# Three output tiles by token halves before the second norm, low parts of its odd tiles on GpSimd, final results written in place

## The chip, the core and the metric

The kernel runs on one core of a Trainium2 chip. The engines are named as in the profile: PE (TensorE, matrix products; PEld is its weight load), DVE (VectorE), ACT (ScalarE), POOL (GpSimd) and SP (SyncE, which issues the DMAs). The metric is the device time of one execution in microseconds (us). Three runs of the kernel before took 1318.2, 1317.3 and 1318.23 us: median 1318.2.

## The reference, cut to what matters

One layer over 512 latent tokens of width 1024 and 256 context tokens: a modulated RMSNorm, two parallel token mixers (a bidirectional state-space scan and windowed attention), a gated merge, then a second modulated RMSNorm and a gated feed-forward with a convolution over tokens, and a final RMSNorm. The change touches the last third:

```python
out_lat = (g_ssd * (y_ssd @ w_o_ssd) + g_att * (y_att @ w_o_att)) @ w_out
x = x + gt1 * out_lat                                   # out stage
h = modulate(x, norm2_g, sh2, sc2)                      # second norm: rmsnorm * (1 + scale) + shift
u = dwconv_centred(h @ w_up, conv_w, conv_b)            # up stage, 2 * 2816 columns
a, b = u[..., :2816], u[..., 2816:]
x = x + gt2 * ((silu(a) * b) @ w_down)                  # down stage
return rmsnorm(x, final_g)                              # final norm
```

An RMSNorm divides each token by the root of the mean square over its 1024 features, so nothing of it can be finished before the last feature of that token is there.

## The kernel before, in words

Activations lie transposed in SBUF: features on the 128 partitions (8 tiles of 128 for width 1024, 22 for 2816), the 512 tokens along the free axis. `HALF` cuts the tokens into two halves of 256.

**Split products.** Each fp32 product is made of three matmuls of rounded parts, high and low: wh·xh, wh·xl, wl·xh (`gemm`, L187, L188, L190, 512 columns each; `half_gemm`, L1073 to L1075, the same for a token half of 256 columns). A weight piece of 512 KB comes by a DMA that SP issues (L140, tile `wraw`, three buffers), ACT rounds it to `whi` (L144) and DVE subtracts for `wlo` (L145), two buffers each. `run` walks a program of steps and loads the pieces one ahead of the step that uses them. `ELSEWHERE` names pieces whose two parts go to a tile of their own; before, that is the out piece 7, in the memory of the dead tile `yh0`.

**Order.** A scheduler orders each engine's instructions; each engine runs its queue in order and waits on semaphores. Where `manual_schedule` stands for PE (`out_last`, `up_step` with t == 0, `down_last`), PE's order is the program's own. Temporaries come from rings of 512-column buffers: `ta` 3, `tb` 2, `tc` 2, `te` 2 (L111). PSUM has three banks `acc` for products and five banks `mis`.

**RMSNorm.** Squares of the tiles are summed on ACT and DVE (`add_square`, or `half_squares` on L1087 for one token half), over partitions by one-column matmuls (`rms_sums`, L229). `rms_root` adds the epsilon (DVE, L237) and takes the power -1/2 (POOL, L238); `rms_spread` copies each token's factor to all partitions by two PE transposes of 128 columns (L244) into a `mis` bank.

**Out stage.** `out_step` makes out tile o for all 512 tokens: x row load into `te` (L1104), product, DVE adds the residual (L1110), square added to `q2`. The steps 0 to 5 are woven with the last six modulation steps. `vectors` follows (small columns, matmuls L464). `out_last` makes tiles 6 and 7 in token halves, in the order o6 and o7 of half 0, o6 and o7 of half 1, with the residual on L1135; the `q2` sums of a half stand behind its o6. The root of half 0 stands behind the k step 5 (counted from 0) of o6 in half 1, the spread of half 0 behind the k step 1 of o7 in half 1.

**Second norm and up step 0.** `norm2_k(k, u)` normalizes tile k of half u: DVE writes xr = x · a · factor into a `tb` buffer (L1145, reads the spread bank in PSUM), ACT writes the high part of xr + shift (L1146), DVE writes the low part (L1147). Up step 0 works tile by tile (`product`, L1185): in half 0 both weight pieces of the step for each k, with the root of half 1 behind k = 3 and its spread behind k = 5; in half 1 first all eight k of the first piece, then all eight of the second. From step 1 on the up steps are plain `gemm`s.

**The end.** `down_last` makes the last down tile in token halves. `finish(u)` scales all eight tiles of half u by the spread factor (DVE, L1244, from PSUM; in half 1 the tiles 5 and 6 on POOL, L1242, from an SBUF copy of the factor that ACT makes on L1236) into `ta` buffers, and SP sends them in five pieces, (0,1), (2,3), (4), (5,6), (7), from L1248. For half 0 that starts beside the last products; for half 1 it is the end of the kernel. L1261 is the last residual.

Of the kernel before, what the change touches and what calls it, by code (L numbers as in the profile page):

```python
# [18 lines left out]
P = 128  # L19
# [20 lines left out]
def raw(ap):  # L40
    return ap.bitcast(F32)
# [3 lines left out]
def tile_hybrid_layer(  # L45
# [67 lines left out]
    def tmp(tag):  # L113
        return tpool.tile([P, 512], F32, tag=tag, name=tag, bufs=TMP[tag])
# [980 lines left out]
    def last_piece():  # L1095
        t = cp.tile([P, 2, 1024], F32R, tag="yh0", name="wlast")
        return t[:, 0, :], t[:, 1, :]

    ELSEWHERE["out", 7] = last_piece

    def out_step(o):
        def fn(w):
# [9 lines left out]

        return [("out", o)], fn

    def out_last(w6, w7):
        xt = [tmp("te") for _ in range(2)]
        for i in range(2):
            nc.sync.dma_start(xt[i], xT[3, :, i * L : (i + 1) * L])
        pf = F["pf"] = misb()
        F["r2"] = []  # L1120

        def root():
            F["rs2"] = half_root(pf, F["sq2"], 0)

        def spread():
            F["r2"].append(rms_spread(F["rs2"], 2))

        with tc.manual_schedule(engines={mybir.EngineType.PE}):
            for u, z in enumerate(HALF):
                for i, w in enumerate((w6, w7)):  # L1130
                    ps = accb()
                    half_gemm(ps, mh, ml, z, w, 8, 0, 8, {} if u == 0 else {1: spread} if i else {5: root})
                    if i == 0:
                        half_sums(pf, q2, u)
                    V.scalar_tensor_tensor(  # L1135
                        x1[1][:, 2 + i, z], ps[:, :HL], g1h[:, 6 + i : 7 + i], xt[i][:, z], ALU.mult, ALU.add
                    )
                F["sq2"] = half_squares([x1[1][:, 2 + i, z] for i in range(2)])

    h2h, h2l = mh, ml  # L1140
# [1 line left out]
    def norm2_k(k, u):  # L1142
        a, s, z = a2[:, k : k + 1], mod2[:, 8 + k : 9 + k], HALF[u]
        xr = tmp("tb")[:, :HL]
        V.scalar_tensor_tensor(xr, x1[k // 4][:, k % 4, z], a, F["r2"][u][:, :HL], ALU.mult, ALU.mult)  # L1145
        S.activation(h2h[:, k, z], xr, AF.Identity, bias=s)  # L1146
        V.scalar_tensor_tensor(h2l[:, k, z], xr, s, raw(h2h[:, k, z]), ALU.add, ALU.subtract)  # L1147

    def close_c1():
        c1pool.close()  # L1150
# [25 lines left out]
    def up_step(t):  # L1176
        def fn(wa, wb):
            pa, pb = accb(), accb()
            if t == 0:

                with tc.manual_schedule(engines={mybir.EngineType.PE}):
                    def product(ps, w, k, u):
                        c, z, st, en = slice(k * P, (k + 1) * P), HALF[u], u == 0 and k == 0, k == KT - 1
                        for v, y in ((0, h2h), (0, h2l), (1, h2h)):
                            T.matmul(  # L1185
                                ps[:, z], w[v][:, c], y[:, k, z],
                                start=st and v == 0 and y is h2h, stop=en and v == 1, skip_group_check=True,
                            )
# [36 lines left out]
    def down_last(*w):  # L1225

        pf = misb()
        for u in range(2):
            half_sums(pf, q3, u)
        scaled, r = {}, {}  # L1230

        def finish(u, r3):
            z = HALF[u]
            if u:
                r3s = tmp("tc")[:, :HL]
                S.copy(r3s, r3[:, :HL])  # L1236

            for cs in ((0, 1), (2, 3), (4,), (5, 6), (7,)):
                t = tmp("ta").rearrange("p (a b) -> p a b", a=2)
                for v, c in enumerate(cs):  # L1240
                    if u and c in scaled:
                        G.tensor_tensor(t[:, v, :], scaled[c], r3s, ALU.mult)  # L1242
                    else:
                        V.scalar_tensor_tensor(  # L1244
                            t[:, v, :], x1[c // 4][:, c % 4, z], col(V_FG, c), r3[:, :HL], ALU.mult, ALU.mult
                        )
                n = len(cs)
                nc.sync.dma_start(out[cs[0] * P : (cs[0] + n) * P, z].rearrange("(a p) t -> p a t", a=n), t[:, :n, :])  # L1248
                if cs[0] == 2:
                    yield  # L1250

        def root():
            r["s"] = half_root(pf, r["sq"], 0)

        def spread():
            r["f"] = finish(0, rms_spread(r["s"], 2))
            next(r["f"])

        def add(u):
            xo = x1[1][:, 3, HALF[u]]  # L1260
            V.scalar_tensor_tensor(xo, ps[u][:, :HL], mod2[:, 31:32], xo, ALU.mult, ALU.add)  # L1261
            r["sq"] = half_squares([xo])

        for i, c in enumerate((5, 6)):
            scaled[c] = tmp("te")[:, :HL]
            S.activation(scaled[c], x1[1][:, c % 4, HALF[1]], AF.Copy, scale=col(V_FG, c))
        ps = [accb(), accb()]
        with tc.manual_schedule(engines={mybir.EngineType.PE}):
# [7 lines left out]
            for _ in finish(1, rms_spread(r["s"], 2)):  # L1276
                pass

    run(
# [92 lines left out]
```

## Time and profile before

| what | value |
|---|---|
| median of three runs | 1318.2 us (1317.3 to 1318.23) |
| the profiled execution's own time | 1317.22 us |
| its span, first to last instruction | 1315.4 us |
| mean granted clock of PE | 0.985 |
| DMA moved | 168.65 MB |
| out tile 5, start of its product | 910.51 us |
| `out_last`, first product | 916.76 us |
| up step 0, first product | 930.34 us |
| up step 1, first product | 949.69 us |
| last residual of half 1 (L1261) | 1303.07 us |

Times within the profile count from the span's start. The busy shares are averages over stages with different limits. A line of a timeline has the start, the duration, the engine, the line of the kernel, the operation, what it writes and reads, its shape, and in brackets the engine's idle time before it and what ended that; "x2" joins two that follow each other. A row of waits has the waiting engine, tile and line, what it waited for, the total in us, how often, and the longest.

### The profile page before, as it was taken

To read this page: it belongs to the slowest core of one execution; us is meant where nothing else is said; L and a number is where in the kernel's file an instruction comes from. 1 tells how busy PE (TensorE), PEld (TensorE's weight loads), DVE (VectorE), ACT (ScalarE), POOL (GpSimd) and SP (SyncE) were. 2 spreads that over 40 slices of the span, in tenths; PEclk is the share of its full clock that TensorE was granted. 3 is DMA by queue.
4 is the path that set the end of the run, shared out by engine and by line. 5 is a ranking of instruction groups with operands and counts; after the bars stand their busy time and mean duration, and the time that the engine had idled before them with its cause. 6 is when DMAs were issued, how large, how long until landed. Compare 5 with 4: busy or idle time off the path is not lost.

```text
span 1315.4 us, 17187 instructions
## 1 busy us (share of the span) xinstructions
PE 1270.1 (97%) x6434; PEld 1028.7 (78%) x6434; DVE 912.7 (69%) x1457; ACT 640.5 (49%) x1182; POOL 133.3 (10%) x104
## 2 busy tenths in 40 slices
PE   4989999999999999999999999999999999999996
PEld 2777777787778878778787787888888888888886
DVE  4578887888666588888888756776677767773333
ACT  4376666666535456475574654223444444442221
POOL 0000000000000024333443430000000000000000
PEclk8998999999999999999999999999999999999998
DMA  7612222211236235444455658767133433333331
GB/s 287 234 33 80 73 80 65 79 67 57 88 112 186 95 93 135 158 112 129 145 123 190 168 166 280 248 204 249 41 116 115 131 104 114 117 110 93 99 89 65
DMA packets 86931, 168.65 MB, mean 128 GB/s; under 512 B 6784, under 2 KB 42112, under 8 KB 86848
## 3 DMA queue, kind: packets, MB, share of 16 engines
q1 hardware_dynamic: 86848, 167.56, 40.9%
q8 instruction: 50, 0.82, 0.3%
q14 instruction: 33, 0.27, 0.1%
HBM read 150.62 MB, written 16.91 MB: 127 GB/s over the span
## 4 chain that ended last, share of the span: by engine, by line
PE 87%; DVE 6%; ACT 3%; issue 1%; DMA 1%; SPq 0%; POOL 0%; DVEq 0%; ACTq 0%; POOLq 0%
PE acc L187 21%; PE acc L188 21%; PE acc L190 21%; PE score L560 2%; PE pt L584 2%; PE mis L924 2%; PE mis L931 2%; PE mis L837 2%; PE po L589 2%; DVE wlo L145 1%; PE po L590 1%; PE mis L855 1%; ACT ta L485 1%; PE mis L765 1%; PE acc L332 1%
## 5 line engine op out<-in xcount | busy, mean ns | idle before, releaser
L145 DVE TENSOR_TENSOR wlo<-wraw,whi 128x1024 fp32r<-128x1024 f32 (+1 forms) x163 | 206.1, 1265 | 133.7 <-ACT whi L144 131.5
L144 ACT CAST whi<-wraw 128x1024 fp32r<-128x1024 f32 (+1 forms) x163 | 168.9, 1037 | 230.5 <-PE acc L188 199.2
L187 PE MATMUL acc<-hlh,whi 128*128 128x512 f32 (+1 forms) x512 | 212.0, 414 | 0.4 <-ACT whi L144 0.4
L190 PE MATMUL acc<-hlh,wlo 128*128 128x512 f32 (+1 forms) x512 | 203.3, 397 | 2.2 <-DVE wlo L145 2.2
L188 PE MATMUL acc<-hll,whi 128*128 128x512 f32 (+1 forms) x512 | 203.5, 398 | 0.0
L187 PE MATMUL acc<-mh,whi 128*128 128x512 f32 x384 | 149.6, 390 | 0.0
L190 PE MATMUL acc<-mh,wlo 128*128 128x512 f32 x384 | 149.4, 389 | 0.0
L188 PE MATMUL acc<-ml,whi 128*128 128x512 f32 x384 | 149.4, 389 | 0.0
L187 PEld LDWEIGHTS acc<-hlh,whi 128*128 128x128 f32 (+1 forms) x512 | 96.7, 189 | 22.1 <-issue 4.1
L190 PEld LDWEIGHTS acc<-hlh,wlo 128*128 128x128 f32 (+1 forms) x512 | 96.3, 188 | 22.1 <-DVE wlo L145 2.9
L188 PEld LDWEIGHTS acc<-hll,whi 128*128 128x128 f32 (+1 forms) x512 | 96.7, 189 | 20.4 <-issue 4.1
L190 PEld LDWEIGHTS acc<-mh,wlo 128*128 128x128 f32 x384 | 72.1, 188 | 15.1
L187 PEld LDWEIGHTS acc<-mh,whi 128*128 128x128 f32 x384 | 72.1, 188 | 15.0
L188 PEld LDWEIGHTS acc<-ml,whi 128*128 128x128 f32 x384 | 72.1, 188 | 14.7
L839 POOL TENSOR_TENSOR st<-st,eT 128x512 f32<-128x512 f32 x24 | 32.8, 1368 | 458.0 <-ACT st L857 444.6
L737 ACT ACTIVATE ta<-acc,half 128x512 f32<-128x512 f32 (+1 forms) x66 | 46.6, 706 | 41.0 <-PE acc L190 41.0
L567 DVE CUSTOM_DVE_ANT_0 p<-score,winm,nsink 128x512 f32<-128x512 f32 (+1 forms) x64 | 52.0, 813 | 18.8 <-PE score L560 17.3
L571 ACT ACTIVATE p<-p,mneg 128x512 f32<-128x512 f32 (+1 forms) x64 | 49.9, 779 | 31.2 <-DVE mneg L567 31.0
L238 POOL TENSOR_TENSOR rs<-ms,phalf 128x2 f32<-128x2 f32 (+1 forms) x7 | 5.5, 790 | 541.0 <-DVE ms L237 541.0
L187 PE MATMUL acc<-fh,whi 128*128 128x512 f32 x154 | 60.0, 390 | 0.0
L190 PE MATMUL acc<-fh,wlo 128*128 128x512 f32 x154 | 59.9, 389 | 0.0
L188 PE MATMUL acc<-fl,whi 128*128 128x512 f32 x154 | 59.9, 389 | 0.0
(309 smaller groups left out, 2766.1 us busy)
## 6 DMA issues: line engine op xcount, KB each, us to landing
wraw<-wup SPq DMA_DIRECT2D x44, 512.0 KB, 3.5
fb<-cs_d SPq DMA_DIRECT2D x32, 512.0 KB, 6.7
wraw<-wm SPq DMA_DIRECT2D x32, 512.0 KB, 3.7
wraw<-wx SPq DMA_DIRECT2D x24, 512.0 KB, 3.6
wm<-wm SPq DMA_DIRECT2D x16, 512.0 KB, 5.5
wraw<-wz SPq DMA_DIRECT2D x16, 512.0 KB, 3.5
wraw<-wg SPq DMA_DIRECT2D x16, 512.0 KB, 3.6
wraw<-wos SPq DMA_DIRECT2D x16, 512.0 KB, 4.7
```

The lines of the kernel that those rows point to most:

```text
L144: S.copy(hi[:, :n], r[:, :n])
L145: V.tensor_tensor(lo[:, :n], r[:, :n], raw(hi[:, :n]), ALU.subtract)
L187: T.matmul(ps, wh, xh[:, k0 + k, :], start=a, stop=False)
L188: T.matmul(ps, wh, xl[:, k0 + k, :], start=False, stop=False)
L190: T.matmul(ps, wl, xh[:, k0 + k, :], start=False, stop=b)
L560: T.matmul(ps[:, o : o + w], Q[h][:, b * P : (b + 1) * P], k[:, j, z[0] * P : z[0] * P + w], start=v == 0 and o % 512 in (0, P), stop=v == ...
L567: V.tensor_tensor_reduce(p[:, :n], ps[:, o0 : o0 + n], m, op0=ALU.add, op1=ALU.min, scale=1.0, scalar=nsink[:, h : h + 1], accum_out=mn,)
L571: S.activation(p[:, :n], p[:, :n], AF.Exp, bias=mn, scale=-1.0, accum_out=den[:, i : i + 1])
L584: T.transpose(pt[:, i * P : (i + 1) * P], pts[i][:, c * P : (c + 1) * P], ident)
L589: T.matmul(po, vst[:, t, j, :], pth, start=c == 0, stop=False)
L737: S.activation(o[:, :n], ps[:, :n], AF.Identity, scale=hcol(base_w, stride + i), bias=hcol(base_b, i))
L839: G.tensor_tensor(h8(n), h8(s), bc64(eT[:, z0 : z0 + 8, c]), ALU.mult)
```

## The change

1. **Out stage.** Out tile 5 leaves the woven steps and joins `out_last`, which now makes o5, o6, o7 of half 0, then o5, o6, o7 of half 1. The three weight pieces lie in tiles of their own (`yh0` to `yh2`). The three x rows are loaded into `ld` buffers. The square of o5 is added to `q2` half by half; the `q2` sums of a half stand behind k = 2 of its o7. The root of half 0 stands behind k = 5 of o5 in half 1, its spread behind k = 4 of o6 in half 1.
2. **Second norm.** For odd k the low part is made by POOL: ACT writes xr + shift a second time, unrounded, into a `ta` buffer (L1159 after), and POOL subtracts the high part (L1160 after). Even k stay on DVE. In up step 0 the order of the three matmuls becomes wh·xh, wl·xh, wh·xl, so the low part is used last.
3. **The end.** The final results are written in place over `x1`, no longer into `ta` buffers, and sent from there. For half 1 the factor is spread twice, into two banks: one for DVE, one for ACT's copy.

On the engines' queues the scheduler follows with: the three out weights one behind the other on SP's queue, the weight splits of o5, o6, o7 and of up step 0 ahead of the first xr, and in half 1 of the norm two xr followed by one low part on DVE.

```diff
-    ELSEWHERE["out", 7] = last_piece
+    for o in (5, 6, 7):
+        ELSEWHERE["out", o] = piece_in("yh%d" % (o - 5))
...
-    def out_last(w6, w7):
-        xt = [tmp("te") for _ in range(2)]
-        for i in range(2):
-            nc.sync.dma_start(xt[i], xT[3, :, i * L : (i + 1) * L])
+    def out_last(*w):
+        xt = [cp.tile([P, L], F32, tag="ld", name="ld", bufs=3) for _ in range(3)]
+        for i, o in enumerate((5, 6, 7)):
+            nc.sync.dma_start(xt[i], xT[o // 2, :, (o % 2) * L : (o % 2 + 1) * L])
...
-                for i, w in enumerate((w6, w7)):
+                for i in range(3):
+                    after = {}
+                    if u == 1:
+                        after = {0: {5: root}, 1: {4: spread}}.get(i, {})
+                    if i == 2:
+                        after[2] = lambda u=u: half_sums(pf, q2, u)
                     ps = accb()
-                    half_gemm(ps, mh, ml, z, w, 8, 0, 8, {} if u == 0 else {1: spread} if i else {5: root})
+                    half_gemm(ps, mh, ml, z, w[i], 8, 0, 8, after)
+                    x = x1[1][:, 1 + i, z]
+                    V.scalar_tensor_tensor(x, ps[:, :HL], g1h[:, 5 + i : 6 + i], xt[i][:, z], ALU.mult, ALU.add)
                     if i == 0:
-                        half_sums(pf, q2, u)
-                    V.scalar_tensor_tensor(
-                        x1[1][:, 2 + i, z], ps[:, :HL], g1h[:, 6 + i : 7 + i], xt[i][:, z], ALU.mult, ALU.add
-                    )
+                        sq = half_squares([x])[0]
+                        V.tensor_tensor(q2[:, z], q2[:, z], sq, ALU.add)
...
-        V.scalar_tensor_tensor(h2l[:, k, z], xr, s, raw(h2h[:, k, z]), ALU.add, ALU.subtract)
+        if k % 2:
+            t = tmp("ta")[:, :HL]
+            S.activation(t, xr, AF.Identity, bias=s)
+            G.tensor_tensor(h2l[:, k, z], t, raw(h2h[:, k, z]), ALU.subtract)
+        else:
+            V.scalar_tensor_tensor(h2l[:, k, z], xr, s, raw(h2h[:, k, z]), ALU.add, ALU.subtract)
...
-                        for v, y in ((0, h2h), (0, h2l), (1, h2h)):
+                        for v, y in ((0, h2h), (1, h2h), (0, h2l)):
...
-        def finish(u, r3):
+        def finish(u):
             z = HALF[u]
+            r3 = rms_spread(r["s"], 2)
             if u:
                 r3s = tmp("tc")[:, :HL]
-                S.copy(r3s, r3[:, :HL])
+                S.copy(r3s, rms_spread(r["s"], 2)[:, :HL])
             for cs in ((0, 1), (2, 3), (4,), (5, 6), (7,)):
-                t = tmp("ta").rearrange("p (a b) -> p a b", a=2)
-                for v, c in enumerate(cs):
+                for c in cs:
+                    x = x1[c // 4][:, c % 4, z]
                     if u and c in scaled:
-                        G.tensor_tensor(t[:, v, :], scaled[c], r3s, ALU.mult)
+                        G.tensor_tensor(x, scaled[c], r3s, ALU.mult)
                     else:
-                        V.scalar_tensor_tensor(
-                            t[:, v, :], x1[c // 4][:, c % 4, z], col(V_FG, c), r3[:, :HL], ALU.mult, ALU.mult
-                        )
+                        V.scalar_tensor_tensor(x, x, col(V_FG, c), r3[:, :HL], ALU.mult, ALU.mult)
...
-        + weave([out_step(o) for o in range(6)], msteps[18:24])
+        + weave([out_step(o) for o in range(5)], msteps[18:24])
...
-        + [([("out", 6), ("out", 7)], out_last), ([], close_c1)]
+        + [([("out", o) for o in (5, 6, 7)], out_last), ([], close_c1)]
```

More of the change, by code (lines that the diff above doesn't have):

```diff
@@ L1093, in half_root, with piece_in, fn @@
         return rms_root(pf[:, 2 * u : 2 * u + 2], 2, EPS)
-    def last_piece():
-        t = cp.tile([P, 2, 1024], F32R, tag="yh0", name="wlast")
-        return t[:, 0, :], t[:, 1, :]
-    ELSEWHERE["out", 7] = last_piece
+    def piece_in(tag):
+        def fn():
+            t = cp.tile([P, 2, 1024], F32R, tag=tag, name="wlast")
+            return t[:, 0, :], t[:, 1, :]
+        return fn
+    for o in (5, 6, 7):
+        ELSEWHERE["out", o] = piece_in("yh%d" % (o - 5))
     def out_step(o):
@@ L1183, in product @@
                         c, z, st, en = slice(k * P, (k + 1) * P), HALF[u], u == 0 and k == 0, k == KT - 1
-                        for v, y in ((0, h2h), (0, h2l), (1, h2h)):
+                        for v, y in ((0, h2h), (1, h2h), (0, h2l)):
                             T.matmul(
                                 ps[:, z], w[v][:, c], y[:, k, z],
-                                start=st and v == 0 and y is h2h, stop=en and v == 1, skip_group_check=True,
+                                start=st and v == 0 and y is h2h, stop=en and y is h2l, skip_group_check=True,
                             )
@@ L1230, in down_last @@
         scaled, r = {}, {}
[L1232 removed]
+        def finish(u):
             z = HALF[u]
+            r3 = rms_spread(r["s"], 2)
             if u:
                 r3s = tmp("tc")[:, :HL]
[L1236 removed]
+                S.copy(r3s, rms_spread(r["s"], 2)[:, :HL])
             for cs in ((0, 1), (2, 3), (4,), (5, 6), (7,)):
[L1239 to L1240 removed]
+                for c in cs:
+                    x = x1[c // 4][:, c % 4, z]
                     if u and c in scaled:
[L1242 removed]
+                        G.tensor_tensor(x, scaled[c], r3s, ALU.mult)
                     else:
[L1244 to L1249 removed]
+                        V.scalar_tensor_tensor(x, x, col(V_FG, c), r3[:, :HL], ALU.mult, ALU.mult)
+                n, c = len(cs), cs[0]
+                nc.sync.dma_start(
+                    out[c * P : (c + n) * P, z].rearrange("(a p) t -> p a t", a=n), x1[c // 4][:, c % 4 : c % 4 + n, z]
+                )
+                if c == 2:
                     yield
@@ L1255, in spread @@
         def spread():
-            r["f"] = finish(0, rms_spread(r["s"], 2))
+            r["f"] = finish(0)
             next(r["f"])
@@ L1275, in down_last @@
             r["s"] = half_root(pf, r["sq"], 1)
-            for _ in finish(1, rms_spread(r["s"], 2)):
+            for _ in finish(1):
                 pass
```

## The prediction

> **What bounds the kernel now.** I read the page first: engine shares, then the chain that ended last.
>
> ```profile
> PE 1270.1 (97%) x6434; PEld 1028.7 (78%) x6434; DVE 912.7 (69%) x1457; ACT 640.5 (49%) x1182; POOL 133.3 (10%) x104
> ...
> PE 87%; DVE 6%; ACT 3%; issue 1%; DMA 1%; SPq 0%; POOL 0%; DVEq 0%; ACTq 0%; POOLq 0%
> ```
>
> PE fills the span; only places where PE waits, or nothing is left for it, can be shortened. The change touches two: the second norm and the very end. The table of stages shows the first (columns: stretch and its length, then busy time and instruction count of PE, PEld, DVE, ACT, POOL, then granted clock, DMA share, GB/s).
>
> ```profile
> 860.00:880.00 20.00, 20.00 (x94) 16.66 (x93) 15.79 (x22) 5.06 (x6) 0.00 (x0) 1.00 0.68 220
> ...
> 930.30:939.80 9.50, 9.02 (x64) 7.71 (x62) 8.05 (x20) 4.62 (x10) 0.70 (x1) 1.00 0.14 52
> 939.80:949.70 9.90, 8.42 (x48) 7.09 (x47) 7.70 (x16) 4.78 (x8) 0.00 (x0) 0.83 0.04 5
> 942.00:944.00 2.00, 1.24 (x7) 0.84 (x7) 1.89 (x6) 1.19 (x3) 0.00 (x0) 1.00 0.00 0
> 944.00:946.00 2.00, 1.99 (x7) 1.68 (x8) 1.34 (x3) 0.66 (x2) 0.00 (x0) 0.54 0.00 0
> 946.00:948.00 2.00, 2.00 (x12) 2.00 (x12) 0.67 (x1) 1.73 (x2) 0.00 (x0) 0.61 0.00 0
> ```
>
> The out stage is PE's (20.00 of 20.00). From 930.3 PE gets 7 matmuls into 2 us where DVE is busy 1.89, and then the clock falls to 0.54 and 0.61. The timeline of PE gives the borders (start, duration, instruction):
>
> ```profile
> 910.51 0.39 PE L187 MATMUL acc<-mh,whi 128*128 128x512 f32 x1
> 915.95 0.95 PE L464 MATMUL mis<-ones,tm 128*128 128x1 f32 x8
> 916.76 0.37 PE L1073 MATMUL acc<-mh,whi 128*128 128x256 f32 x1
> 930.22 0.28 PE L1075 MATMUL acc<-mh,wlast 128*128 128x256 f32 x1
> 930.34 0.28 PE L1185 MATMUL acc<-mh,whi 128*128 128x256 f32 x1
> 933.65 0.95 PE L229 MATMUL mis<-rmsc,tc 128*128 128x1 f32 x8
> 934.46 0.36 PE L1185 MATMUL acc<-mh,whi 128*128 128x256 f32 x1
> 936.40 0.38 PE L244 MATMUL mis<-ident,rs 128*128 128x128 f32 x2
> 946.45 0.41 PE L1185 MATMUL acc<-ml,whi 128*128 128x256 f32 x1
> 946.66 0.41 PE L1185 MATMUL acc<-mh,wlo 128*128 128x256 f32 x1
> 949.69 0.40 PE L187 MATMUL acc<-mh,whi 128*128 128x512 f32 x1
> ```
>
> A 512-column matmul takes (915.95 - 910.51)/24 = 0.227 us, a 256-column one 930.34 - 930.22 = 0.12. Up step 0 has 96 of the latter, 11.5 us, plus 0.8 for the sums (933.65 to 934.46) and 0.2 for the spread: 12.5 us of work. It takes 949.69 - 930.34 = 19.35, so 6.8 us are lost here. About 1.4 of it is the clock: some 15 matmuls between 944.1 and 947.5 stand about 0.215 apart (946.45 to 946.66) instead of 0.12. The rest is waiting. For what, the waits of that stretch and the timelines of DVE and ACT say:
>
> ```profile
> PEld acc L1185 <- DVE ml L1147: 4.0, 10, 0.5
> ...
> 927.97 1.23 DVE L145 TENSOR_TENSOR wlo<-wraw,whi 128x1024 fp32r<-128x1024 f32 x1 [0.48 <-ACT whi L144]
> 929.12 0.87 DVE L1145 SCALAR_TENSOR_TENSOR tb<-x,a,mis 128x256 f32<-128x256 f32 x2
> 937.59 0.48 DVE L1145 SCALAR_TENSOR_TENSOR tb<-x,a,mis 128x256 f32<-128x256 f32 x1
> 940.32 0.48 DVE L1145 SCALAR_TENSOR_TENSOR tb<-x,a,mis 128x256 f32<-128x256 f32 x1
> 940.72 0.48 DVE L1147 SCALAR_TENSOR_TENSOR ml<-tb,mod,mh 128x256 fp32r<-128x256 f32 x1
> 945.10 0.49 DVE L1147 SCALAR_TENSOR_TENSOR ml<-tb,mod,mh 128x256 fp32r<-128x256 f32 x1 [0.24 <-ACT mh L1146]
> ...
> 940.90 0.51 ACT L1146 ACTIVATE mh<-tb,mod 128x256 fp32r<-128x256 f32 x1 [0.41 <-DVE tb L1145]
> ```
>
> PE waits for DVE's low part; DVE makes a tile in (940.32 - 937.59)/3 = 0.91 us, of which its two instructions take 0.40 each start to start (940.32 to 940.72). The norm's first tile starts 1.2 us before PE needs it (929.12 against 930.34), behind a weight split of 1.23 us.
>
> **Part by part.** All sums stand against the profiled execution: 1317.22 us, span 1315.4. The median is 1318.2, 0.98 more; I add that difference at the end.
>
> *Three tiles in halves.* o5 becomes 48 matmuls of 0.12 instead of 24 of 0.227: 5.74 for 5.44, **+0.3**. The extra square's add is a 0.4 us DVE instruction in a stage where DVE has over 4 us of 20 free. Three splits and three row loads move earlier, and SP's three out weights now follow each other, where each used to wait for a split. Two rows bound what that can cost (SP's issue of the last out weight, and the median landing time of all four):
>
> ```profile
> 908.11 0.33 SPq L140 DMA_DIRECT2D wraw<-wout x1
> ...
> wraw<-wout SPq DMA_DIRECT2D x4, 512.0 KB, 4.1
> ```
>
> Issued no earlier than now, o7's weight would land at 912.2 and be cast and split (1.2 each) by 914.6; its first half starts at 911.4 + 2 x 2.9 = 917.1. o5's and o6's stand one and two issues ahead of it and are needed 5.7 and 2.9 earlier. No cost; if that cover fails, PE stands still for as long as the piece is late, one for one.
>
> *Start of the norm.* The half-0 spread now stands after the fifth of eight k steps of o6's second half. Behind it PE has 9 + 24 matmuls, 33 x 0.12 = 4.0 us, before up step 0. With 0.3 from spread to first xr, and no split in between (all are issued earlier), the norm leads by about 4.3 us instead of 1.2. Half 0 of up step 0 then meets finished tiles and runs at PE's pace: 5.74 + 0.8 + 0.2 = 6.8 us from 930.6, to 937.5. The sums and root of half 1 come earlier too: I lay its spread at 935.1 and its first xr at 935.4, against 937.59 now.
>
> *Low parts of odd tiles on POOL.* DVE goes from four instructions per pair to three (1.2 us), ACT from two to three (0.41 + 0.51 spacing above, about 1.25). With two xr buffers the pair's round trip decides: xr to its cast 0.58 (940.32 to 940.90), the cast 0.55, the low part and the next xr 0.53 more: 1.66 us a pair instead of 1.83. POOL's subtract of this shape is not in the norm of before, but there is one at the end:
>
> ```profile
> L1242 POOL TENSOR_TENSOR ta<-te,tc 128x256 f32<-128x256 f32 x2 | 1.4, 724 | 4.5 <-DMA out<-ta 4.5
> ...
> 519.66 2.31 DVE L145 TENSOR_TENSOR wlo<-wraw,whi 128x1024 fp32r<-128x1024 f32 x1
> ...
> 520.97 2.16 POOL L938 TENSOR_TENSOR dx<-dx,te 128x512 f32<-128x512 f32 x1
> ```
>
> I take 0.72 (same shape); the ends are 0.5 (DVE's own 0.48) and 2.16, the 512-wide one under contention. At 0.72 the last low part is ready at 935.4 + 3 x 1.66 + 2.7 (xr, two casts, third ACT instruction, POOL) = 943.0, against 945.6 now. The new product order puts the low part last in each k, so PE works on the high part meanwhile. After it come one matmul and the other weight's 24: 943.0 + 0.2 + 2.9 = **946.1, against 949.69: 3.6 us gained**. That supposes full clock. The half-1 stretch still gives PE only six matmuls a pair, 0.72 us of 1.66 against 0.72 of 1.83 now, so I hold the fall of the clock for as likely as not; it takes back 1.4, leaving 2.2. What is late next: the next up weight, whose cast waits until PE has left this one; cast and split end about 0.5 us ahead of need. The following stage is PE's, so the gain is kept.
>
> Where DVE and POOL meet, the trace shows a price: the split at 519.66 took 2.31 instead of 1.23, and POOL's instruction 2.16. The Trainium skill ("SBUF — State Buffer", Who interferes with whom) says that a DVE instruction with two SBUF inputs contends with a GpSimd instruction that reads SBUF, by an exclusive lock; these rows agree. By that rule the xr (one input in PSUM) is spared and an even low part can be held by a POOL one; in my layout they alternate, so the sum by the rule is the same.
>
> *The end.* The timeline of the last microseconds, and a row of the DMA view (kilobytes and median us to landing):
>
> ```profile
> 1302.40 10.15 SPq L1248 DMA_DIRECT2D out<-ta  x10
> 1305.82 0.58 PE L244 MATMUL mis<-ident,rs 128*128 128x128 f32 x2 [1.10 <-POOL rs L238]
> 1306.49 0.37 ACT L1236 COPY tc<-mis 128x256 f32<-128x256 f32 x1 [2.43 <-PE mis L244]
> 1306.90 0.87 DVE L1244 SCALAR_TENSOR_TENSOR ta<-x,vec,mis 128x256 f32<-128x256 f32 x2 [0.70 <-ACT tc L1236]
> 1308.11 1.26 DVE L1244 SCALAR_TENSOR_TENSOR ta<-x,vec,mis 128x256 f32<-128x256 f32 x3 [0.34 <-DMA out<-ta]
> 1310.23 1.41 POOL L1242 TENSOR_TENSOR ta<-te,tc 128x256 f32<-128x256 f32 x2 [4.46 <-DMA out<-ta]
> 1311.28 0.48 DVE L1244 SCALAR_TENSOR_TENSOR ta<-x,vec,mis 128x256 f32<-128x256 f32 x1 [1.91 <-DMA out<-ta]
> ...
> out<-ta SPq DMA_DIRECT2D x4, 128.0 KB, 2.0
> ```
>
> POOL idles 4.46 us and DVE 1.91 until a transfer frees a ta buffer. In place there is no buffer to wait for. DVE no longer waits for ACT's copy either, which reads a bank of its own; the second spread costs PE about 0.25 us that only ACT's copy sees. The four in-place products of half 0 that now precede the root's first step cost it 0.2. After: DVE's six from 1306.7, the last done at 1306.7 + 5 x 0.4 + 0.5 = 1309.2; POOL's two from about 1307.4, done at 1308.9. SP holds (5,6) second, so the later three issues follow 1308.9 at 0.44 each: the last starts at about 1310.0 instead of 1312.1. Three pieces leaving so close together cost about 0.2 of backlog. Gain **1.9** (bounds: 1.3 if POOL pays 1.0 each, 2.2 with no backlog).
>
> **Sum.** 3.6 + 1.9 = 5.5 without the fall of the clock, 2.2 + 1.9 = 4.1 with it: 1311.7 or 1313.1 against the profiled execution, 1312.7 or 1314.1 against the median. I forecast the middle, **1313.5**.
>
> **Rivals.**
> 1. *The norm stays as slow.* DVE and POOL meet after all, and each POOL instruction holds DVE for its 0.72: 4 x 0.72 = 2.9 us off the 3.6, and with the fall of the clock nothing is left. Only the end gains: 1318.2 - 1.9 - (0 to 0.7) = 1315.6 to 1316.3. For it: the 2.31 us split. Against: the alternation, and the earlier start of half 0, which this doesn't touch. A piece of the out weights 2 us late would give the same.
> 2. *POOL becomes the norm's bound* (the slower side). Its four subtracts of half 1 lie in the chain to PE. Up to about 1.6 us each they hide in the pair's 1.66; at 1.7 the norm's gain is gone, at 2.16 it ends 3.8 us late, and the whole is +1.9 over the median (1320.1). Beyond 0.2% slower it is from about 2.25 each; at 2.5 the norm is 7.4 late: 1318.2 + 7.4 - 1.9 = 1323.7. For it: 2.16 at 520.97. Against: that one has twice the columns, and 0.72 stands in this very shape.
> 3. *The end gives nothing* (it is bound by transfers, not by buffers): 1314.6 to 1316.0. For it: ten pieces leave within 10 us. Against: POOL's 4.46 us of waiting, and the last transfers take 2.0 like the others.
>
> **Chances.** Forecast 0.72; rival 1 0.14, rival 2 0.06, rival 3 0.08. About 0.2% (2.6 us) is what a measurement of this kernel can tell from no change, so faster is below 1315.6 and slower above 1320.8. Faster: 0.72, half of rival 1's lower end (0.03), most of rival 3 (0.06): 0.81. Same: 0.14. Slower: most of rival 2, 0.05. The range runs from 1311.4 (no fall of the clock, 2.2 at the end, and a little of the 0.98) to 1316.4, which takes in rivals 1 and 3.
>
> **What would show it.** Half 0 of up step 0 without gaps, from about 930.6 to 937.5; its first xr some 4 us ahead of PE; xr two by two about 1.66 us apart in half 1; POOL's subtracts near 0.72; up step 1 at 946 (full clock) or 947.5; no wait on out transfers at the end, and the last one issued near 1310 less the earlier gain. Wrong it would be if POOL's subtracts took over 1.6, if out_last showed PE waiting for a weight's split, or if the span's end moved less than up step 1 did.

## The result, and the profile after

The changed kernel takes 1312.06 us (median of five runs, 1311.62 to 1314.08) against 1318.2 us: ratio 0.996, 95% interval 0.9945 to 0.9974 (a ratio here is taken over all runs and is not the quotient of the two medians). In the last series below eight more runs of the same kernel gave 1313.1 against 1317.9 us: 0.9966 (0.9956 to 0.9976). The profiled execution took 1312.06 us with a span of 1310.3, 5.1 less than before. The forecast was 1313.5 with a range of 1311.4 to 1316.4.

Where the 5.1 us went is read from PE's borders, the same as in the prediction. PE's timeline of the changed kernel:

```profile
910.58 0.95 PE L464 MATMUL mis<-ones,tm 128*128 128x1 f32 x8
...
911.38 0.37 PE L1073 MATMUL acc<-mh,wlast 128*128 128x256 f32 x1
...
930.71 0.28 PE L1200 MATMUL acc<-mh,whi 128*128 128x256 f32 x1
...
937.56 0.28 PE L1200 MATMUL acc<-mh,whi 128*128 128x256 f32 x1
...
946.30 0.40 PE L187 MATMUL acc<-mh,whi 128*128 128x512 f32 x1
```

The out stage up to up step 0 takes 930.71 - 910.58 = 20.13 with o5 in it; before it was 930.34 - 910.51 = 19.83: +0.30. Up step 0 takes 946.30 - 930.71 = 15.59 instead of 19.35: -3.76. From up step 1 to the last residual nothing changes: 1299.66 - 946.30 = 353.36 (row below) against 353.38. From that residual to the span's end it is 10.64 instead of 12.33: -1.69. The rest of the 5.1 is a shift of 0.07 ahead of the stage.

Up step 0 in the table of stages (stretch and length, busy time and count of PE, PEld, DVE, ACT, POOL, granted clock, DMA share, GB/s):

```profile
930.70:937.60 6.90, 6.90 (x61) 6.90 (x60) 4.19 (x12) 4.06 (x10) 2.65 (x5) 1.00 0.00 0
937.60:946.30 8.70, 7.25 (x50) 6.09 (x49) 5.25 (x11) 5.66 (x11) 2.90 (x4) 1.00 0.01 2
942.00:944.00 2.00, 1.54 (x11) 1.20 (x10) 0.08 (x1) 0.72 (x2) 0.72 (x1) 1.00 0.03 8
944.00:946.00 2.00, 2.00 (x19) 2.00 (x18) 1.28 (x2) 1.37 (x2) 0.00 (x0) 1.00 0.00 0
```

Half 0 has no gap; half 1 still has some, and DVE is no longer busy throughout (5.25 of 8.70). The clock stays at 1.00, where it fell to 0.54 before. The timelines of DVE, ACT and POOL, POOL's group, and the waits of that stretch:

```profile
926.53 0.87 DVE L1155 SCALAR_TENSOR_TENSOR tb<-x,a,mis 128x256 f32<-128x256 f32 x2 [0.56 <-PE mis L244]
935.62 0.87 DVE L1155 SCALAR_TENSOR_TENSOR tb<-x,a,mis 128x256 f32<-128x256 f32 x2 [1.13 <-PE mis L244]
937.19 0.87 DVE L1155 SCALAR_TENSOR_TENSOR tb<-x,a,mis 128x256 f32<-128x256 f32 x2
938.84 0.87 DVE L1155 SCALAR_TENSOR_TENSOR tb<-x,a,mis 128x256 f32<-128x256 f32 x2
942.44 0.72 POOL L1160 TENSOR_TENSOR ml<-ta,mh 128x256 fp32r<-128x256 f32 x1 [0.91 <-ACT ta L1159]
...
L1160 POOL TENSOR_TENSOR ml<-ta,mh 128x256 fp32r<-128x256 f32 x8 | 5.9, 732 | 10.3 <-ACT ta L1159 10.3
...
PEld acc L1200 <- POOL ml L1160: 2.3, 4, 0.7
```

The first xr stands 930.71 - 926.53 = 4.2 ahead of the up step (1.2 before). In half 1 the pairs follow each other by 1.65 (937.19 to 938.84), POOL takes 0.73 and itself waits for ACT, and PE now waits for POOL's low parts, 2.3 us in four waits. The end (last residual, spreads, products, issues of DMAs):

```profile
1298.99 8.68 SPq L1262 DMA_DIRECT2D out<-x  x10
1299.66 0.48 DVE L1277 SCALAR_TENSOR_TENSOR x<-acc,mod,x 128x256 f32<-128x256 f32 x1
1302.67 1.11 PE L244 MATMUL mis<-ident,rs 128*128 128x128 f32 x4 [1.36 <-POOL rs L238]
1303.39 2.44 DVE L1260 SCALAR_TENSOR_TENSOR x<-x,vec,mis 128x256 f32<-128x256 f32 x6 [1.62 <-PE mis L244]
1303.87 0.37 ACT L1253 COPY tc<-mis 128x256 f32<-128x256 f32 x1 [3.22 <-PE mis L244]
1304.32 1.41 POOL L1258 TENSOR_TENSOR x<-te,tc 128x256 f32<-128x256 f32 x2 [1.71 <-ACT tc L1253]
```

POOL's wait of 4.46 and DVE's of 1.91 for out transfers are gone; DVE runs its six products without a stop. What SP waits for is now POOL:

```profile
SPq L1262 <- POOL x L1258: 1.0, 1, 1.0
```

### The profile page after: what moved, and what is told of

It is laid out like the page before. It is cut to its first block, busy times and chain, and to the rows that moved or that the text cites. A ratio compares the mean times of both kernels' runs of the same rounds, so it can differ in the third digit from the quotient of the medians.

```text
span 1310.3 us, 17244 instructions
## 1 busy us (share of the span) xinstructions
PE 1267.6 (97%) x6460; PEld 1028.8 (79%) x6460; DVE 909.3 (69%) x1451; ACT 643.0 (49%) x1191; POOL 139.4 (11%) x112
## 4 chain that ended last, share of the span: by engine, by line
PE 87%; DVE 6%; ACT 4%; DMA 1%; issue 1%; POOL 0%; SPq 0%; DVEq 0%; ACTq 0%; POOLq 0%
PE acc L188 21%; PE acc L187 21%; PE acc L190 21%; PE score L560 2%; PE pt L584 2%; PE mis L924 2%; PE mis L931 2%; PE mis L837 2%; PE po L589 2%; DVE wlo L145 2%; PE po L590 1%; PE mis L855 1%; PE mis L765 1%; ACT ta L485 1%; PE acc L1073 1%
## 5 line engine op out<-in xcount | busy, mean ns | idle before, releaser
L145 DVE TENSOR_TENSOR wlo<-wraw,whi 128x1024 fp32r<-128x1024 f32 x161 | 203.7, 1265 | 134.8 <-ACT whi L144 132.6
L144 ACT CAST whi<-wraw 128x1024 fp32r<-128x1024 f32 x161 | 166.7, 1036 | 218.6 <-PE acc L188 181.6
L188 PE MATMUL acc<-ml,whi 128*128 128x512 f32 x376 | 146.4, 389 | 0.3 <-DVE ml L1042 0.3
L187 PE MATMUL acc<-mh,whi 128*128 128x512 f32 x376 | 146.5, 390 | 0.0
L190 PE MATMUL acc<-mh,wlo 128*128 128x512 f32 x376 | 146.3, 389 | 0.0
```

The source lines that it names most:

```text
L144: S.copy(hi[:, :n], r[:, :n])
L145: V.tensor_tensor(lo[:, :n], r[:, :n], raw(hi[:, :n]), ALU.subtract)
L187: T.matmul(ps, wh, xh[:, k0 + k, :], start=a, stop=False)
L188: T.matmul(ps, wh, xl[:, k0 + k, :], start=False, stop=False)
L190: T.matmul(ps, wl, xh[:, k0 + k, :], start=False, stop=b)
```

## The experiments

The theory behind the prediction has two halves, the norm and the end. Within the norm two readings were open: that the earlier start carries the gain (A), or POOL's relief of DVE (B). Twelve kernels were run, in three series of four; each series has its own runs of the kernel before. Since executions of one kernel spread over 1.4 to 5 us, the stages of one profile tell more than the medians do, but each kernel has one profile only (the changed kernel two); "up step 0" is the time from its first matmul to that of up step 1, "the end" that from the last residual to the span's end. PE's clock matters at the end too: in the profiles of "only three halves", "only POOL low parts", "no POOL low parts", "(5,6) last", "both of these" and "one spread" it held until the spreading transposes were done, in the others it had fallen to 0.50 by then or fell during them. At a fallen clock the changed kernel's code for the end took 10.57 to 11.09, so ends are compared at like clock.

| kernel | median (runs) | before | ratio, 95% interval | up step 0 | the end |
|---|---|---|---|---|---|
| only three halves | 1314.73 (11) | 1317.45 | 0.9983 (0.9974 to 0.9992) | 16.14 | 11.79 |
| only POOL low parts | 1314.53 (11) | 1317.45 | 0.9978 (0.9969 to 0.9987) | 16.78 | 12.09 |
| only the end | 1315.95 (11) | 1317.45 | 0.9987 (0.9978 to 0.9995) | 19.24, clock falls | 10.95 |
| no POOL low parts | 1314.29 (6) | 1317.45 | 0.9969 (0.9958 to 0.9981) | 18.36, clock falls | 10.07 |
| POOL twice | 1312.92 (5) | 1318.09 | 0.9956 (0.9942 to 0.997) | 16.60 | 10.58 |
| POOL thrice | 1319.66 (11) | 1318.09 | 1.0011 (1.0002 to 1.0019) | 23.46, clock falls | 10.60 |
| interleaved | 1312.41 (5) | 1318.09 | 0.9955 (0.9943 to 0.9968) | 14.05 + 0.79 | 10.57 |
| (5,6) last | 1311.69 (5) | 1318.09 | 0.9953 (0.994 to 0.9965) | 15.59 | 9.66 |
| both of these | 1311.68 (5) | 1317.9 | 0.9959 (0.9946 to 0.9971) | 14.03 + 0.79 | 9.75 |
| no halves | 1313.82 (6) | 1317.9 | 0.9969 (0.9957 to 0.9981) | 16.78 | 11.09 |
| one spread, (5,6) last | 1313.4 (5) | 1317.9 | 0.9968 (0.9955 to 0.998) | 15.60 | 10.11 |
| changed, again | 1313.1 (8) | 1317.9 | 0.9966 (0.9956 to 0.9976) | 15.59 | 10.62 |

**1. Only the three halves** (the first part of the change on the kernel before, all of `out_last` and the program's lines):

```diff
...
-        + weave([out_step(o) for o in range(6)], msteps[18:24])
+        + weave([out_step(o) for o in range(5)], msteps[18:24])
...
```

> Only the three out tiles in token halves; the second norm's low parts all on VectorE with the old product order, the end as before. Theory A (the norm's earlier start carries most of the gain, POOL's share is small): the first xr of half 0 leads up step 0 by about 4.3 us, that half has no stall, half 1 starts near 935.4 plus whatever the out stage moved and needs 8 x 0.91 us a tile, so up step 1 starts 2.7 to 3.2 us earlier relative to the last whole out tile than before, 1.4 less if the clock falls: 1315 to 1316.5 us. Theory B (POOL's relief of VectorE carries the gain): up step 1 moves by under 1 us, 1317.5 us or more.

**2. Only the low parts on POOL** (with the new product order):

```diff
+        if k % 2:
+            t = tmp("ta")[:, :HL]
+            S.activation(t, xr, AF.Identity, bias=s)
+            G.tensor_tensor(h2l[:, k, z], t, raw(h2h[:, k, z]), ALU.subtract)
...
```

> Only the low parts of odd tiles on POOL and the new product order; two out tiles in halves and the end as before. Theory A: the norm starts as late as before (about 1.2 us ahead of the up step), half 0 still stalls on its first tiles, the gain is 0.5 to 1.5 us: 1316.7 to 1317.7 us. Theory B: 2.5 us or more, below 1315.7 us. In both POOL's subtracts take 0.73 each.

Up step 0 took 16.14 and 16.78 (PE's timelines of the two kernels, first the halves, then POOL):

```profile
930.60 0.28 PE L1195 MATMUL acc<-mh,whi 128*128 128x256 f32 x1
...
946.74 0.40 PE L187 MATMUL acc<-mh,whi 128*128 128x512 f32 x1
```

```profile
930.36 0.28 PE L1190 MATMUL acc<-mh,whi 128*128 128x256 f32 x1
...
947.14 0.40 PE L187 MATMUL acc<-mh,whi 128*128 128x512 f32 x1
```

In neither did the clock fall, and before it did, so the price of that fall comes out first. The prediction put it at 1.4 by counting every slow product. But up to the low part of the last tile PE waited for the norm in any case; only what stands behind that product adds to the time. Its row before, and in the kernel with the halves at full clock:

```profile
945.72 0.50 PE L1185 MATMUL acc<-ml,whi 128*128 128x256 f32 x1
```

```profile
943.59 0.32 PE L1195 MATMUL acc<-ml,whi 128*128 128x256 f32 x1
```

From there to up step 1 it is 949.69 - 945.72 = 3.97 before and 946.74 - 943.59 = 3.15 at full clock. The fall cost 0.8, not 1.4, and at full clock the 19.35 of before would be about 18.5. In up step 0 the earlier start alone is then worth 2.4, POOL with the new order alone 1.7. Neither A nor B holds: both parts count, and since the two together reach 15.59, 2.9 less, they overlap by 1.2. Not all of the 2.4 is gained: in the profile of the halves the out stage took 20.64 instead of 19.83, of which 0.3 is the halves and the rest a wait that experiment 9 explains. That leaves 1.6 for the halves and 1.7 for POOL's part.

The medians fell by more, 2.7 and 2.9 us. By the expectations' own limits the 2.7 would speak for A and the 2.9 (2.5 or more) for B, which exclude each other. That the rest is a clock that falls less often fits, but is not shown.

**3. Only the end:**

```diff
...
-                        G.tensor_tensor(t[:, v, :], scaled[c], r3s, ALU.mult)
+                        G.tensor_tensor(x, scaled[c], r3s, ALU.mult)
...
```

> Only the end: results in place, factor spread twice. Theory A and B: no wait for out transfers is left, from the last residual to the span's end 1.7 us less than before: 1316.3 to 1316.7 us. Rival (the end is bound by transfers, not by buffers): within 0.4 us of before.

The median is 1.5 us lower, the end 1.4 shorter (the clock fell at the end in both profiles). POOL's products (DVE's last residual above them) now follow ACT's copy and wait for no transfer:

```profile
1305.25 0.48 DVE L1262 SCALAR_TENSOR_TENSOR x<-acc,mod,x 128x256 f32<-128x256 f32 x1
...
1309.85 1.41 POOL L1243 TENSOR_TENSOR x<-te,tc 128x256 f32<-128x256 f32 x2 [1.71 <-ACT tc L1238]
```

The buffers, not the transfers, held the end. The 1.7 expected was 0.3 too much.

**4. The changed kernel with all low parts on DVE:**

```diff
-        if k % 2:
+        if False:
             t = tmp("ta")[:, :HL]
```

> The changed kernel with every low part on VectorE (three halves, new product order and the new end stay). Theory A: half 1 of the norm needs 0.91 us a tile instead of 0.82, up step 1 starts 0.3 to 0.8 us later than in the changed kernel (1.4 more if the clock falls): 1312.4 to 1314.2 us. Theory B: about 3 us later, 1315 us or more.

The ratio (0.9969) lies inside the intervals of the changed kernel's two series, so the runs don't part the two; the median of 1314.29 lies just above A's range. The profile does part them: up step 0 takes 2.8 longer. This profile had a fall of the clock, and shows its price (the same table of stages):

```profile
942.00:944.00 2.00, 1.49 (x7) 1.17 (x7) 1.75 (x5) 0.91 (x2) 0.00 (x0) 0.64 0.00 0
944.00:946.00 2.00, 2.00 (x10) 2.00 (x10) 0.26 (x1) 0.83 (x1) 0.00 (x0) 0.50 0.03 8
946.00:948.00 2.00, 2.00 (x11) 2.00 (x11) 1.75 (x2) 0.89 (x2) 0.00 (x0) 0.50 0.00 0
```

The kernel with the three halves alone has the same norm on DVE, with the old product order, and took 16.14 without a fall: about 2.2 of the 2.8 is the clock, and 0.55 is what POOL's low parts and the new order are worth together on top of the halves. No run parts these two. An estimate from the pair of tiles ahead of the fall gives the order 0.1 to 0.2 of it: from the first product of the pair to its last it is 0.98 here (941.48 to 942.46) and 1.15 with the halves alone (940.69 to 941.84).

**5 and 6. POOL's subtract written twice and three times** (same values, one after the other):

```diff
+            for _ in range(2):   # 3 in the second kernel
-            G.tensor_tensor(h2l[:, k, z], t, raw(h2h[:, k, z]), ALU.subtract)
+                G.tensor_tensor(h2l[:, k, z], t, raw(h2h[:, k, z]), ALU.subtract)
```

> The changed kernel, with each POOL subtract of the norm written twice (1.46 us an odd tile instead of 0.73; same result). The prediction's rule for POOL (hidden up to about 1.6 us, the gain of the norm gone at 1.7, because the pair's round trip of 1.64 covers it and only the last one shows in full): up step 1 starts 1.5 to 2.5 us later than in the changed kernel, about 1314 us. Rival (POOL and VectorE shut each other out of SBUF when they meet, as at 519.66): VectorE's low parts and POOL's subtracts stretch well beyond 0.48 and 0.73, and up step 1 comes 4 us or more later, 1316 us or more.

> The changed kernel, with each POOL subtract written three times (2.2 us an odd tile). POOL is then the norm's bound: four pairs of half 1 at 2.2 instead of 1.64, and half 0 runs late too. By the prediction's rule up step 1 starts 7 to 8 us later than in the changed kernel: 1319 to 1320.5 us, slower than before. If POOL were off the path, under 1314 us.

POOL's queue in half 1, and the low part of DVE's that it held longest (the kernel with two, then the one with three):

```profile
939.01 6.59 POOL L1161 TENSOR_TENSOR ml<-ta,mh 128x256 fp32r<-128x256 f32 x8 [1.01 <-ACT ta L1159]
```

```profile
935.24 12.14 POOL L1161 TENSOR_TENSOR ml<-ta,mh 128x256 fp32r<-128x256 f32 x15
...
936.86 1.04 DVE L1163 SCALAR_TENSOR_TENSOR ml<-tb,mod,mh 128x256 fp32r<-128x256 f32 x1 [0.19 <-ACT mh L1156]
```

Twice: 6.59/4 = 1.65 a tile is just the pair's period, POOL has no pause left, and up step 0 grows by 1.0, less than the 1.5 to 2.5 expected; what shows is the longer last tile. Thrice: 3 x 12.14/15 = 2.43 a tile, POOL is the bound, up step 0 grows by 7.9 and the kernel is slower than before by 1.6 us. But this profile has a fall of the clock: from the last low part's product to up step 1 it took 952.91 - 947.44 = 5.47, in the changed kernel 946.30 - 943.22 = 3.08. So 2.4 of the 7.9 is the clock and 5.5 is POOL's, and that the 7 to 8 us expected came out is luck. The rival on the slower side was right as a mechanism, and its point of decision, put at 2.25 a tile, lies between these two kernels.

DVE and POOL do meet here. One low part of DVE's in this half takes 1.04 instead of 0.48, the other three 0.53, 0.48 and 0.52. Beside these three it is POOL that waits: its subtracts that start during them take 0.79, 0.87 and 0.91 instead of 0.73. The second of them:

```profile
940.74 0.48 DVE L1163 SCALAR_TENSOR_TENSOR ml<-tb,mod,mh 128x256 fp32r<-128x256 f32 x1 [0.25 <-ACT mh L1156]
...
940.94 0.87 POOL L1161 TENSOR_TENSOR ml<-ta,mh 128x256 fp32r<-128x256 f32 x1
```

**7. Half 1 interleaved:** the second weight's products between those of the first, one k behind.

```diff
                         norm2_k(k, 1)
                         product(pa, wa, k, 1)
-                    for k in range(KT):
-                        product(pb, wb, k, 1)
+                        if k:
+                            product(pb, wb, k - 1, 1)
+                    product(pb, wb, KT - 1, 1)
```

> The changed kernel, with the second weight's products of half 1 put between those of the first, one k behind, instead of after them. PE then works in the gaps of the norm: its last matmul of up step 0 comes about 2 us earlier, but the next weight's cast (1.05) and split (1.23) still wait until the first weight's last product, so that up step 1 starts near the cast's end and its third matmul waits for the split: 0.5 to 0.9 us gained, and the granted clock stays at 1.00 in every 2 us of the stretch: 1311 to 1311.6 us. If the gaps weren't on the path: no gain.

PE's gaps are filled (the table of stages; 17 matmuls where the changed kernel has 11), and what is late next is what was foreseen, the next weight's cast and split (PE's timeline):

```profile
942.00:944.00 2.00, 2.00 (x17) 1.84 (x15) 0.00 (x0) 0.70 (x2) 0.75 (x1) 1.00 0.00 0
```

```profile
930.58 0.28 PE L1200 MATMUL acc<-mh,whi 128*128 128x256 f32 x1
...
944.63 0.50 PE L187 MATMUL acc<-mh,whi 128*128 128x512 f32 x1 [0.42 <-ACT whi L144]
944.97 0.40 PE L188 MATMUL acc<-ml,whi 128*128 128x512 f32 x1
945.89 0.51 PE L190 MATMUL acc<-mh,wlo 128*128 128x512 f32 x1 [0.53 <-DVE wlo L145]
```

The third matmul of up step 1 comes 0.92 after the second instead of two spacings of 0.23 after the first: 0.79 is lost again of the 1.54 gained, which leaves 0.75. The median, 1312.41, lies above the 1311 to 1311.6 expected and doesn't show it.

**8. (5,6) last on SP's queue.** The program's order of the last five pieces, kept by hand:

```diff
-            for cs in ((0, 1), (2, 3), (4,), (5, 6), (7,)):
+            for cs in ((0, 1), (2, 3), (4,), (7,), (5, 6)) if u else ((0, 1), (2, 3), (4,), (5, 6), (7,)):
...
-        with tc.manual_schedule(engines={mybir.EngineType.PE}):
+        with tc.manual_schedule(engines={mybir.EngineType.PE, mybir.EngineType.SP}):
```

> The changed kernel, with SyncE's last five issues in the order (0,1), (2,3), (4), (7), (5,6) instead of (5,6) second. If the wait for POOL's two products behind which three pieces stand is what the end waits for: the last issue comes about 0.9 us earlier, the end 0.5 to 0.9 us: 1311.2 to 1311.6 us. If the transfers themselves bound the end: no difference.

The end is 0.98 shorter than in the changed kernel's profile. SP's and PE's timelines:

```profile
1299.37 7.71 SPq L1262 DMA_DIRECT2D out<-x  x10
1300.04 0.48 DVE L1277 SCALAR_TENSOR_TENSOR x<-acc,mod,x 128x256 f32<-128x256 f32 x1
1303.05 0.65 PE L244 MATMUL mis<-ident,rs 128*128 128x128 f32 x4 [1.36 <-POOL rs L238]
1306.69 0.39 SPq L1262 DMA_DIRECT2D out<-x  x1
```

The last issue starts 6.65 after the residual instead of 7.61. But about half of this is PE's clock, not the order: the four spreading transposes took 0.65 here and 1.11 in the changed kernel's profile, whose clock had by then fallen to 0.50, and ACT's copy and POOL's products stand behind them. The kernel of experiment 4 has (5,6) second and its clock held at the end, so it is the one to compare with (its last residual starts at 1303.13):

```profile
1306.07 0.65 PE L244 MATMUL mis<-ident,rs 128*128 128x128 f32 x4 [1.29 <-POOL rs L238]
...
1310.22 0.41 SPq L1262 DMA_DIRECT2D out<-x  x1
```

Its last issue starts 7.09 after the residual and its end is 10.07. At equal clock the order is therefore worth 0.44 in the last issue and 0.4 in the end, and that the 0.5 to 0.9 expected came out is luck: the other half is a clock that held. In the last issue's place SP itself is the limit now: its five issues start 4.38 to 6.65 after the residual, the last four about 0.50 apart, and POOL is done at 5.61.

**9. Both of these together.**

> The interleaved half 1 of the norm and SyncE's last issues with (5,6) last, together. The two gains lie at different ends of the feed-forward and add: about 0.5 at up step 1, about 0.9 from the last residual to the span's end, so 1.0 to 1.5 us less than the changed kernel in the same call, about 1310.9 us. Rival (a later queue eats the first): no more than (5,6) last gives alone.

Both stage gains are there again (14.03 + 0.79, and 9.75, at a clock that held at the end), 1.4 us in the median of the same series, but the intervals of the two kernels lie over each other, so a version that beats the changed kernel is likely and not shown. Its profile also shows a wait that the prediction had not priced (PE's waits in the out stage, and the timelines of PE and DVE):

```profile
PE mis L229 <- DVE q L1147: 0.8, 1, 0.8
...
919.22 0.58 PE L229 MATMUL mis<-rmsc,q 128*128 128x1 f32 x4 [0.75 <-DVE q L1147]
...
913.32 1.22 DVE L145 TENSOR_TENSOR wlast<-wraw,wlast 128x1024 fp32r<-128x1024 f32 x1 [2.11 <-ACT wlast L144]
```

The last out weight landed late, its split stood at 913.32 instead of 911.57, and behind it on DVE's queue stand two more splits and the new add of o5's square, for which the sums wait. Here the out stage took 1.0 us longer than in the changed kernel (21.14). The same wait stands in two more profiles, that of the halves alone (20.64, 0.5 longer) and that of (5,6) last (20.53, 0.4 longer); four others took 0.1 to 0.2 longer without a wait that the rows name, and the two profiles of the changed kernel (20.13 and 20.14) and that with POOL thrice have none of it.

**10. The changed kernel without the halves:**

```diff
...
-        + [([("out", o) for o in (5, 6, 7)], out_last), ([], close_c1)]
+        + [([("out", 6), ("out", 7)], out_last), ([], close_c1)]
...
```

> The changed kernel without the three halves: o5 stays whole, the norm starts as late as before; POOL's low parts, the product order and the new end stay. If the earlier start is worth what the profile of the three-halves kernel alone says (up step 1 36.8 after the small sums, against 36.6 for POOL's part alone and 35.7 for both), the two overlap: about 0.9 us more than the changed kernel, 1313 us. If the earlier start carried most of the gain: 2.5 us more or over.

Up step 0 took 16.78, as with POOL's part alone: 1.19 more, less the 0.30 of the halves is 0.9. Alone the earlier start was worth 2.4 in up step 0, so 1.2 of it overlaps with POOL's part here too. The medians of the series differ by 0.7, which their intervals don't resolve.

**11. One spread instead of two** (on the kernel with (5,6) last):

```diff
-                S.copy(r3s, rms_spread(r["s"], 2)[:, :HL])
+                S.copy(r3s, r3[:, :HL])
```

> The kernel with (5,6) last, but with one spread of half 1's factor, read by VectorE and by ScalarE's copy from the same bank, as before the change. VectorE's first product waits for the copy again: it starts about 0.45 us later after the last residual, and the span's end comes 0.3 to 0.5 us later after that residual than with two spreads (9.7 us). In the median no difference that can be told.

```profile
1306.42 0.37 ACT L1253 COPY tc<-mis 128x256 f32<-128x256 f32 x1 [2.54 <-PE mis L244]
...
1306.83 2.44 DVE L1260 SCALAR_TENSOR_TENSOR x<-x,vec,mis 128x256 f32<-128x256 f32 x6 [1.83 <-ACT tc L1253]
```

DVE waits for ACT's copy; its first product stands 1306.83 - 1302.89 = 3.94 after the residual instead of 3.48, and the end is 0.45 longer (10.11 against 9.66). This holds with (5,6) last. In the changed kernel, with (5,6) second, SP waits for POOL, and POOL's first product stands 3.98 after the residual with one spread and 4.20 with two, so there the second spread may cost rather than gain; that was not run.

**12. The changed kernel again.**

> The changed kernel unaltered, on the same chip as the other three, and for a second profile. 1311.5 to 1313 us. Up step 1 stands 35.7 us after the small sums if the clock holds, up to 37.1 if it falls; POOL's subtracts 0.73.

35.73 after the small sums (912.38 to 948.11), up step 0 15.59 to the hundredth, no fall of the clock in that stage. The median, 1313.1, lies just above the 1311.5 to 1313 expected.

## Why the prediction was right, point by point

- *Halves of o5, +0.3:* measured 0.30. "No cost" for the earlier splits held in both profiles of the changed kernel, but three of the other kernels with the halves paid 0.4 to 1.0 us there; experiment 9 shows where the step was thin. It compared each weight with its own first matmul; the add of o5's square, behind the splits on DVE's queue, has less slack.
- *Start of the norm:* lead 4.2 (4.3), half 0 from 930.71 to 937.56 without gaps (930.6 to 937.5), first xr of half 1 at 935.62 (935.4).
- *POOL:* 0.73 (0.72), pairs 1.65 (1.66), last low part at 943.16 (943.0), up step 1 at 946.30 (946.1). The gain to up step 1 was 3.4 (3.6, or 2.2 with a fall of the clock). What the number says needs care: part of it is that this execution's clock did not fall where that of before did. The prediction sized that fall wrongly, at 1.4: it counted products that PE would have waited between anyway, and the rows of experiments 1 and 2 leave 0.8. At equal clock the gain is 3.4 - 0.8 = 2.6. The 2.2 for a fall in both was not met by any profile of the changed kernel, and its 1.4 is no fixed price: without POOL's low parts the fall cost about 2.2, with POOL thrice 2.4.
- *The fall of the clock* was held for as likely as not. Of the 14 profiles it came in four, before, only the end, no POOL low parts, and POOL thrice, and in neither of the changed kernel's profiles. In the kernel with POOL twice PE had as few matmuls (the table of stages, 6 in 2 us) and the clock held, so sparse work alone doesn't decide it:

```profile
940.00:942.00 2.00, 0.98 (x6) 0.77 (x6) 1.68 (x5) 1.67 (x5) 1.92 (x3) 1.00 0.00 0
942.00:944.00 2.00, 0.98 (x6) 0.77 (x6) 1.27 (x3) 1.47 (x4) 1.92 (x3) 1.00 0.00 0
```

  How often it falls in either kernel stays open; no run here counts it.
- *The end, 1.9:* measured 1.69, at a clock that had fallen in both profiles. SP's issues behind POOL's pieces, in the changed kernel:

```profile
1305.76 0.37 SPq L1262 DMA_DIRECT2D out<-x  x1
...
1307.27 0.40 SPq L1262 DMA_DIRECT2D out<-x  x1
```

  The last issue starts 7.61 after the residual, where the sum had 1310.0 - 1303.07 = 6.93. The mis-sized term is SP's. The sum's own terms, 1308.9 and three issues at 0.44, give 1310.2, not 1310.0; the issues then stood 0.50 apart (1.51 in all), and POOL was done 0.24 later, the spreads standing at half clock. So the last issue came 1.45 earlier than before, where the sum had 2.1. The other 0.24 of the 1.69 is the last transfer, which landed 3.03 after its issue and 3.27 before; since that time ranges from 2.9 to 3.5 over the 14 profiles, neither a gain nor the sum's 0.2 of backlog can be told from it, and the nearness of 1.69 to 1.9 is in part luck. That (5,6) second holds the end by 0.4 is shown by experiments 4 and 8, that the buffers held it before by experiment 3.
- *Rival 1* (DVE and POOL meet) did not occur: 0.73 and 0.48 are undisturbed, since the two alternate. The Trainium skill ("SBUF — State Buffer", Who interferes with whom) has the one that comes second blocked for the other's whole instruction; in experiment 6, where they overlap, the trace agrees on who waits but not on how long. POOL comes second three times and is longer each time (0.79, 0.87 and 0.91 for 0.73), by 0.14 less than what was left of DVE's instruction; in the fourth meeting the two start within 0.02 and DVE waits (1.04 for 0.48).
- *Rival 2* occurs with POOL thrice, not before, and its prices were too high. At 1.65 a tile (POOL twice) 1.0 of the 3.4 was lost, where the prediction had the whole gain gone at 1.7. At 2.43 its line from 3.8 late at 2.16 to 7.4 late at 2.5 gives 6.7; from the start of the stretch that holds o5 and the small sums to up step 1 the kernel with POOL thrice took 43.60 against 39.18 before, 4.4 more.
- *Rival 3* fell with experiment 3.
- *The number.* 1312.06 is 6.1 below the median of before, and 1.4 below the forecast; in the last series the same two kernels are 4.8 apart, where the forecast had 4.7. The 0.98 by which the median of before lay over its profiled execution was added to the forecast, but the profiled execution of the changed kernel is its median. So how near the forecast came is in part a matter of how executions spread, not of the mechanism.

## What to carry to other kernels

An engine that waits on a short chain between two dense stages is helped twice: by starting the chain earlier under the last products of the stage ahead, and by shortening its round trip; the two overlap, so each is sized with the other in place. A ring of buffers that transfers must empty can be the bound of a kernel's last microseconds, and after it the order of the issues can be; a piece that waits for the slowest engine goes last. Where single executions spread by more than the change is worth, the same two events in each profile measure it, and a clock that fell in only one of them is taken out first, at the price of the products behind the last wait alone. Two ends or two stages at different clocks are not a comparison: half of what (5,6) last seemed to gain was a clock that held.

## What was not expected of the hardware

One fall of PE's clock in a stretch of gaps cost 0.7 us (only the end: 951.89 - 948.02 = 3.87 behind the last low part's product, against 3.15), 0.8 (before), about 2.2 (no POOL low parts) and 2.4 (POOL thrice), as much as either part of the change. PE's clock at the very end was 0.50 in the changed kernel's profile and 1.00 in that of (5,6) last; the four transposes of 128 columns took 1.11 and 0.65, and POOL's first product stood 4.66 and 4.20 after the residual. POOL's subtract of 128x256 cost 0.73 alone, and one every 0.81 when it followed itself without a pause (12.14 / 15).
